# Summing the attention's two output halves in DRAM with an adding transfer

## The chip, the cores and the metric

The kernel runs on one core of a Trainium2 chip. Its engines are TensorE (PE in the profile; PEld is its weight load), VectorE (DVE), ScalarE (ACT), GpSimd (POOL) and SyncE (SP); each works through its own instructions in the order in which the program lists them, and waits on semaphores for the others. Sixteen DMA engines move data; SP and POOL issue the transfers, each on a queue of its own. The metric is the device time of one execution in microseconds, taken as the median of several runs.

## What is computed

One block of a sequence model on 1024 positions of width 1024: a norm, an input projection, two mixers (an mLSTM and a sparse attention, "NSA"), their gated sum through two branch weights, an output projection, and a gated feed-forward part. The change touches the result of the attention and the place where it is used:

```python
def block(i):                      # 64 queries t, 8 heads in 2 groups
    ...
    p_c = masked_softmax(lc, cmp_end[None, :] <= t[:, None])    # compressed keys
    o_c = jnp.einsum('bgrqc,bgcd->bgrqd', p_c, vc_)
    ...
    p_s = masked_softmax(ls, mask_s[:, :, None])                # selected blocks
    o_s = jnp.einsum('bgrqn,bgqnd->bgrqd', p_s, v_g)
    ...
    p_w = masked_softmax(lw, mask_w)                            # window of 512
    o_w = jnp.einsum('bgrqk,bgkd->bgrqd', p_w, v_wb)
    return gb[..., 0:1] * o_c + gb[..., 1:2] * o_s + gb[..., 2:3] * o_w

y_n = nsa_mixer(...)
ys = jnp.stack([y_m, y_n], axis=2)
branch = jnp.einsum('btnw,nwd->btnd', ys, w_branch[l])
mixed = jnp.sum(jax.nn.sigmoid(merge) * branch, axis=2)
```

## The kernel before

All matrix products work on numbers that are split in two: a rounded high part (made on ACT) and the rest, the low part (made by a subtraction on DVE or POOL). A product of two split operands takes three matmuls (`mm3`, L351 to L353).

**The attention** (names in the trace: S, E, T, obank, os) runs over 32 units: four head pairs p, and in each eight tiles i of 128 queries. Unit 13, for example, is tile 5 of pair 1, and unit 16 the first of pair 2. For each unit and each of the two heads, PE forms the logits (S16w and S16s are the window and block logits of unit 16; L1430, L1431), DVE adds the bias and takes the row extremes (L1457), ACT takes the exponential (L1461), and DVE or ACT scales (L1482). The compressed keys have a tile of their own, E16c for unit 16, whose unused columns POOL fills with zeros (L1449) before PE transposes it. PE transposes all of it in groups (T, L1512), ACT and DVE split them (TH, TL), and PE multiplies with the values, accumulating in obank (L1532, L1534). The values are stored as 64 columns of high parts beside 64 columns of low parts, so the accumulated output of a unit is a tile of 128 partitions, of which partitions 0 to 63 hold the product with the high parts and partitions 64 to 127 the one with the low parts. The result is the sum of the two halves, which lie on different partitions.

At the end of a unit ACT copies this tile to the output tile os (L1540; two buffers in turn), and SP stores its halves into two DRAM arrays, d_yn[0][p] and d_yn[1][p] (L1542). The order of the work on PE, ACT and DVE comes from a planner in the kernel, which places operations by estimated costs; POOL and SP simply get their instructions as the planner emits the operations that issue them. When the last logits of a pair are done, `load_pair` issues the loads for the next pair: q on POOL's queue (L1286, L1287; tiles S), on every second pair k too (L1294; tiles R and S, followed by two copies, L1282), and the bias rows on SP's queue (L1301, from d_rep). PE fills its spare time in the attention with dense tiles of the merge gates (d, L351 to L353), whose weights are split into whi on ACT (L331) and wlo on POOL (L333), and whose results ACT evicts (mg, L1387).

**The branch inputs.** Behind the attention, `load_y` (L1814 to L1826) brings eight inputs of 128 x 1024 for the branch products, two transfers each into a ring of six buffers: for k below 4 the mLSTM's output and its gate, which DVE multiplies, and for k of 4 to 7 the two attention halves, which DVE adds (L1820). Each input is then split into YH (ACT, L347) and YL (DVE, L348). This runs beside the last three dense tiles; step k issues the loads of input k and works on input k - 2. Behind the dense tiles PE forms the branch products (br), which need all of YH and YL and the branch weights, of which the first is split (whi, wlo) in the midst of this work. Later stages (output projection, feed-forward part) come from a second planner, and nothing in them is touched.

Of the kernel before, what the change touches and what calls it, by code (L numbers as in the profile page):

```python
# [11 lines left out]
ALU = mybir.AluOpType  # L12
PSUM = bass.MemoryType.PSUM

P = 128
# [26 lines left out]
def cast32(ap):  # L42
    return ap.bitcast(F32)
# [129 lines left out]
def body(ctx, tc, a, out):  # L173
    nc = tc.nc
# [111 lines left out]
    d_so = [tc.dram_tile([P, T], F32, name=f"d_so{j}") for j in range(4)]  # L286
    d_ym = [tc.dram_tile([P, T], F32, name=f"d_ym{j}") for j in range(4)]
    d_yn = [[tc.dram_tile([P, T], F32, name=f"d_yn{z}{j}") for j in range(4)] for z in range(2)]
# [57 lines left out]
    def split_evict(hi, lo, src):  # L346
        nc.scalar.activation(hi, src, AF.Copy)  # L347
        nc.vector.tensor_tensor(lo, src, cast32(hi), ALU.subtract)  # L348

    def mm3(ps, ah, al, bh, bl, first, last):  # L350
        nc.tensor.matmul(ps, ah, bh, start=first, stop=False)  # L351
        nc.tensor.matmul(ps, ah, bl, start=False, stop=False)  # L352
        nc.tensor.matmul(ps, al, bh, start=False, stop=last)  # L353
# [917 lines left out]
    def vhl(i, n):  # L1271
        return vat(4 * i + n)
# [119 lines left out]
    with ExitStack() as sc:  # L1392
# [97 lines left out]
        def t_groups(u):  # L1490
            p, i = units[u]
            bl = [(2, k) for k in range(nwin(i))]
            gr = [(0, bl[z:z + 2]) for z in range(0, len(bl), 2)] + [(0, [(0, 0)])]
            bl = [(1, k) for k in range(i + 1)]
            gr += [(1, bl[z:z + 2]) for z in range(0, len(bl), 2)]
            return gr
# [4 lines left out]
        def t_job(u, gi, grp, last):  # L1501

            p, i = units[u]
            g = p // 2
            if gi == 0:
                PO[u] = [None, 0, sum(len(x[1]) for x in t_groups(u))]
            m = len(grp)
            pt = psC.tile([P, 2, 2 * P], F32, name=f"T{u}_{gi}", tag="T", bufs=2)
            for z, (b, kb) in enumerate(grp):
                for r in range(2):  # L1510
                    e = EX[u, "c"][:, r, :] if b == 0 else EX[u, "w" if b == 2 else "s", r][:, P * kb:P * kb + P]
                    nc.tensor.transpose(pt[:, z, P * r:P * r + P], e, ident)  # L1512
            hl = []

            def high():
                hl.append(cp.tile([P, 2, 2 * P], F32R, name=f"TH{u}_{gi}", tag="TH", bufs=NTH))
                nc.scalar.activation(hl[0][:, 0:m], pt[:, 0:m], AF.Copy)  # L1517

            def low():
                hl.append(cp.tile([P, 2, 2 * P], F32R, name=f"TL{u}_{gi}", tag="TL", bufs=NTH))  # L1520
                nc.vector.tensor_tensor(hl[1][:, 0:m], pt[:, 0:m], cast32(hl[0])[:, 0:m], ALU.subtract)  # L1521

            def pv():
                th, tl = hl
                st = PO[u]
                po = obank[:, u % 2, :]
                for z, (b, kb) in enumerate(grp):
                    if b == 0:
                        vv = VHC[:, g, :]
                    else:  # L1530
                        vv = vhl(kb + (max(0, i - 4) if b == 2 else 0), 2 * (b - 1) + g)
                    nc.tensor.matmul(po, vv, th[:, z, :], start=(st[1] == 0), stop=False)  # L1532
                    st[1] += 1
                    nc.tensor.matmul(po, vv, tl[:, z, :], start=False, stop=(st[1] == st[2]))  # L1534
                if last:
                    os_ = cp.tile([P, 256], F32, name=f"os{u}", tag="os", bufs=2)

                    def out_copy():

                        nc.scalar.activation(os_, po, AF.Copy)  # L1540
                        for z in range(2):
                            nc.sync.dma_start(d_yn[z][p].rearrange("(r d) t -> d r t", r=2)[:, :, P * i:P * i + P],  # L1542
                                              os_[64 * z:64 * z + 64, :].rearrange("d (r t) -> d r t", r=2))
                    return out_copy
                return None

            return 2 * m * 107.0, high, low, pv
# [122 lines left out]
        def ready(op, eng):  # L1670
            t = 0.0
            for d in op.deps:
                d = dep_op(d)
                if isinstance(d, tuple):
                    e = pair_at.get(d[1])
                else:
                    e = d.end
                    if e is not None and d.eng != eng:
                        e += LAT
                if e is None:  # L1680
                    return None
                t = max(t, e)
            if op.extra is not None and len(talloc) >= 2:
                e = talloc[-2].end
                if e is None:
                    return None
                t = max(t, e + LAT)
            return t
# [31 lines left out]
        while any(queues.values()):  # L1720
            best = None
            for e in queues:
                cand = None
                for op in queues[e][:LOOK[e]]:
                    r = ready(op, e)
# [31 lines left out]
            if e == "DVE" and op in s_free:  # L1757
                p = units[op.prio[0]][0]
# [13 lines left out]
    def q1_tile(n, dt):  # L1772
        if n not in q1 or q1[n].dtype != dt:
            q1[n] = q1p.tile([P, 4, 512], dt, name=f"q1_{n}_{len(q1)}", tag=f"q1_{n}", bufs=1)
        return q1[n]
# [24 lines left out]
    with ExitStack() as se:  # L1800
        dp = se.enter_context(tc.tile_pool(name="stD", bufs=1, reuse_waits="tile"))
        psD = se.enter_context(tc.tile_pool(name="psD", bufs=1, space=PSUM, reuse_waits="tile"))
        YH = dp.tile([P, 8, T], F32R, name="YH")
        YL = dp.tile([P, 8, T], F32R, name="YL")
        def load_y():

            ring = [q1_tile(n, F32)[:, 2 * z:2 * z + 2, :].rearrange("p a c -> p (a c)") for n in (4, 0, 1) for z in range(2)]
            ys, loads = {}, 0
            for k in range(10):
                ys[k] = []  # L1810
                for src in ([d_ym[k], d_so[k]] if k < 4 else [d_yn[0][k - 4], d_yn[1][k - 4]]) if k < 8 else []:
                    ys[k].append(ring[loads % 6])
                    loads += 1
                    nc.sync.dma_start(ys[k][-1], src[:, :])  # L1814
                if k > 1:
                    y, *more = ys.pop(k - 2)
                    if k < 6:
                        nc.scalar.activation(more[0], more[0], AF.Sigmoid)
                    for y2 in more:
                        nc.vector.tensor_tensor(y, y, y2, ALU.mult if k < 6 else ALU.add)  # L1820
                    for half in range(2):
                        hs = slice(512 * half, 512 * half + 512)
                        split_evict(YH[:, k - 2, hs], YL[:, k - 2, hs], y[:, hs])
                yield

        ly = load_y()  # L1826
        for j in range(MG1, 16):
            for z, _ in enumerate(merge_tile(j, gring, psD, 8)):
                if z % 4 == 1:
                    next(ly, None)  # L1830
        for _ in ly:
            pass
        for d in range(8):
            n = j_br[d]
            wh, wl = ws.get(n)
            for half in range(2):
                hs = slice(512 * half, 512 * half + 512)
                sg = []
                for b in range(2):
                    gg = gring.tile()  # L1840
                    nc.sync.dma_start(gg, d_mg[8 * b + d][:, hs])
                    nc.scalar.activation(gg, gg, AF.Sigmoid)
                    sg.append(gg)
                for b in range(2):
                    ps = psD.tile([P, 512], F32, name=f"br{d}{half}{b}", tag="D", bufs=8)
                    for k in range(4):
                        kk = 4 * b + k
                        mm3(ps, wh[:, kk, :], wl[:, kk, :], YH[:, kk, hs], YL[:, kk, hs], k == 0, k == 3)
                    nc.vector.tensor_tensor(sg[b], ps, sg[b], ALU.mult)
                if d < 7 and half == 0:  # L1850
                    ws.dma(n + 2)
                    ws.split(n + 1)
                if d == 6 and half == 1:
                    ws.split(n + 2)
                if d == 7:
                    ws.split(n + 3 if half == 0 else n + 4)
                nc.vector.tensor_tensor(sg[0], sg[0], sg[1], ALU.add)
                split_evict(UTH[:, d, hs], UTL[:, d, hs], sg[0])
# [385 lines left out]
    for gi, pairs in enumerate(GROUPS):  # L2244
        ra, rb = {}, {}
        for z in range(2):
            for p in pairs:
                t = 2 * p + z
                ra[p, z] = load2(d_gu[t][:, :], [gub[t]])
                rb[p, z] = load2(wdn[P * t:P * t + P, :])  # L2250
        for q in QS:
# [32 lines left out]
            for j in range(4):  # L2284
                d = acc[q, j]
# [18 lines left out]
    for r in (1, 0):  # L2304
        for j in range(4):
            i = 2 * j + r
# [69 lines left out]
```

## Time and profile before

| | us |
|---|---|
| median of 3 runs (1571.67 to 1578.49) | 1574.69 |
| the profiled execution | 1576.46 |
| its span, first to last instruction | 1574.7 |
| PE busy | 1529.6 |
| DVE busy | 1175.1 |
| ACT busy | 782.0 |
| POOL busy | 126.7 |

The span is 1.8 us shorter than the profiled execution, which has some time around its first and last instruction. The mean granted clock of TensorE over the span is 0.991 of full speed.

In rows of a timeline the first number is the start in us from the span's start, the second the busy time, then engine, line, operation, and output <- inputs; in brackets stands the idle time before it and what ended it. Rows of waits give total us, how often, and the longest. Rows of transfers give their number, the KB of one and the median us from issue to landing.

### The profile page before, as it was taken

To read this page: it belongs to the slowest core of one execution; us is meant where nothing else is said; L and a number is where in the kernel's file an instruction comes from. 1 tells how busy PE (TensorE), PEld (TensorE's weight loads), DVE (VectorE), ACT (ScalarE), POOL (GpSimd) and SP (SyncE) were. 2 spreads that over 40 slices of the span, in tenths; PEclk is the share of its full clock that TensorE was granted. 3 is DMA by queue.
4 is the path that set the end of the run, shared out by engine and by line. 5 is a ranking of instruction groups with operands and counts; after the bars stand their busy time and mean duration, and the time that the engine had idled before them with its cause. 6 is when DMAs were issued, how large, how long until landed. Compare 5 with 4: busy or idle time off the path is not lost.

```text
span 1574.7 us, 22067 instructions
## 1 busy us (share of the span) xinstructions
PE 1529.6 (97%) x7714; PEld 1291.2 (82%) x7714; DVE 1175.1 (75%) x2467; ACT 782.0 (50%) x1668; POOL 126.7 (8%) x184
## 2 busy tenths in 40 slices
PE   6999999998999999998999999999999999999998
PEld 5877888886989888986888888888888888888876
DVE  6978888855888688856564597666666666978996
ACT  6325665653788688865443253333333333454443
POOL 2000000022111211001000041000000000000120
PEclk9999999999999999999999999999999999999999
DMA  8424655599142914137556222222322223650202
GB/s 272 125 75 135 214 182 155 176 241 233 40 112 54 172 40 113 48 101 254 153 176 206 75 67 87 80 81 84 132 92 81 81 88 127 253 215 0 107 1 107
DMA packets 162839, 198.21 MB, mean 126 GB/s; under 512 B 9944, under 2 KB 121974, under 8 KB 162728
## 3 DMA queue, kind: packets, MB, share of 16 engines
q1 hardware_dynamic: 150840, 183.06, 36.5%
q0 software_dynamic: 11600, 13.09, 5.0%
q8 instruction: 61, 1.00, 0.3%
q10 hardware_dynamic: 288, 0.66, 0.1%
q14 instruction: 50, 0.41, 0.1%
HBM read 146.34 MB, written 58.29 MB: 130 GB/s over the span
## 4 chain that ended last, share of the span: by engine, by line
PE 85%; DVE 7%; DMA 5%; ACT 2%; issue 1%; SPq 0%; POOL 0%; DVEq 0%; ACTq 0%; POOLq 0%
PE PS L352 15%; PE PS L353 15%; PE PS L351 15%; PE bk L351 4%; PE bk L352 4%; PE bk L353 4%; PE T L1512 4%; PE obank L1534 2%; PE d L351 2%; PE obank L1532 2%; PE d L353 2%; PE d L352 2%; PE br L353 2%; PE br L351 2%; PE br L352 2%; DMA d_ql<-S 1%
## 5 line engine op out<-in xcount | busy, mean ns | idle before, releaser
L1877 DVE TENSOR_TENSOR sl<-PS,sl 128x512 f32<-128x512 f32 x182 | 123.0, 687 | 99.7 <-PE PS L353 97.7
L1521 DVE TENSOR_TENSOR TL<-T,TH 128x512 fp32r<-128x512 f32 (+1 forms) x184 | 103.3, 582 | 29.1 <-ACT TH L1517 28.3
L1517 ACT ACTIVATE TH<-T 128x512 fp32r<-128x512 f32 (+1 forms) x184 | 90.2, 510 | 28.7 <-PE T L1512 25.7
L1880 ACT ACTIVATE sl<-sl 128x512 f32<-128x512 f32 (+1 forms) x85 | 53.3, 631 | 71.7 <-PE PS L352 46.3
L1877 DVE TENSOR_TENSOR sl<-sl,sl 128x512 f32<-128x512 f32 (+1 forms) x111 | 75.2, 686 | 15.4 <-ACT sl L1880 11.8
L351 PE MATMUL bk<-UTH,op 128*128 128x512 f32 x192 | 77.5, 403 | 1.6 <-ACT S L779 1.6
L1880 ACT ACTIVATE wh<-sl 128x512 fp32r<-128x512 f32 x61 | 38.5, 631 | 81.5 <-PE PS L352 69.1
L353 PE MATMUL bk<-UTH,op 128*128 128x512 f32 x192 | 75.1, 391 | 0.0
L352 PE MATMUL bk<-UTL,op 128*128 128x512 f32 x192 | 75.0, 391 | 0.0
L351 PE MATMUL d<-UTH,whi 128*128 128x512 f32 x176 | 71.9, 409 | 1.4 <-ACT mg L1387 0.7
L353 PE MATMUL d<-UTH,wlo 128*128 128x512 f32 x176 | 69.3, 394 | 1.4 <-POOL wlo L333 1.4
L352 PE MATMUL d<-UTL,whi 128*128 128x512 f32 x176 | 69.1, 393 | 0.0
L351 PE MATMUL PS<-q 128*128 128x512 f32 x172 | 67.0, 390 | 0.0
L352 PE MATMUL PS<-q 128*128 128x512 f32 x172 | 67.0, 390 | 0.0
L353 PE MATMUL PS<-q 128*128 128x512 f32 x172 | 67.0, 390 | 0.0
L1880 ACT ACTIVATE q<-sl 128x512 fp32r<-128x512 f32 x74 | 43.3, 624 | 45.9 <-PE PS L352 30.1
L351 PE MATMUL bk<-T,op 128*128 128x512 f32 x144 | 58.3, 405 | 0.0
L353 PE MATMUL bk<-T,op 128*128 128x512 f32 x144 | 56.4, 391 | 0.0
L352 PE MATMUL bk<-T,op 128*128 128x512 f32 x144 | 56.3, 391 | 0.0
L351 PE MATMUL br<-YH,whi 128*128 128x512 f32 x128 | 50.8, 397 | 2.2 <-ACT whi L331 2.2
L353 PE MATMUL br<-YH,wlo 128*128 128x512 f32 x128 | 50.8, 397 | 2.2 <-POOL wlo L333 2.2
L1877 DVE TENSOR_TENSOR wh<-sl,wh 128x512 fp32r<-128x512 f32 x58 | 39.7, 685 | 15.3 <-ACT wh L1880 15.3
(1377 smaller groups left out, 4854.6 us busy)
## 6 DMA issues: line engine op xcount, KB each, us to landing
rp<-in_w_in SPq DMA_DIRECT2D x22, 512.0 KB, 4.6
ra<-in_w_gate SPq DMA_DIRECT2D x22, 512.0 KB, 4.0
d_gu<-sl SPq DMA_DIRECT2D x44, 256.0 KB, 2.0
q<-d_mg SPq DMA_DIRECT2D x32, 256.0 KB, 2.9
d_rep<-d_row SPq DMA_DIRECT2D x8, 960.0 KB, 7.4
sl<-d_gu SPq DMA_DIRECT2D x15, 512.0 KB, 5.3
sl<-in_w_down SPq DMA_DIRECT2D x15, 512.0 KB, 4.3
ra<-in_w_up SPq DMA_DIRECT2D x11, 512.0 KB, 3.5
```

The source lines that it names most:

```text
L351: nc.tensor.matmul(ps, ah, bh, start=first, stop=False)
L352: nc.tensor.matmul(ps, ah, bl, start=False, stop=False)
L353: nc.tensor.matmul(ps, al, bh, start=False, stop=last)
L1512: nc.tensor.transpose(pt[:, z, P * r:P * r + P], e, ident)
L1517: nc.scalar.activation(hl[0][:, 0:m], pt[:, 0:m], AF.Copy)
L1521: nc.vector.tensor_tensor(hl[1][:, 0:m], pt[:, 0:m], cast32(hl[0])[:, 0:m], ALU.subtract)
L1532: nc.tensor.matmul(po, vv, th[:, z, :], start=(st[1] == 0), stop=False)
L1534: nc.tensor.matmul(po, vv, tl[:, z, :], start=False, stop=(st[1] == st[2]))
L1877: return pl.step(alts, lambda e: ENG[e].tensor_tensor(out_(), x(), y(), alu), reads, writes, **kw)
L1880: return pl.step((("ACT", cost),), lambda e: nc.scalar.activation(out_(), x(), fn), reads, writes, **kw)
```

## The change

The two stores of a unit now go to the same array, d_yn[0][p]. The first half is stored by SP as before. The second half is sent by POOL's queue with an accumulating transfer, which adds to what lies in DRAM. Since it reads and writes what the first has written, it waits until that has landed. `load_y` then loads one array for each attention input instead of two, and there is nothing left to add on DVE.

```diff
                         for z in range(2):
-                            nc.sync.dma_start(d_yn[z][p].rearrange("(r d) t -> d r t", r=2)[:, :, P * i:P * i + P],
-                                              os_[64 * z:64 * z + 64, :].rearrange("d (r t) -> d r t", r=2))
+                            kw = {"accum_op": ALU.add} if z else {}
+                            (nc.gpsimd if z else nc.sync).dma_start(d_yn[0][p].rearrange("(r d) t -> d r t", r=2)[:, :, P * i:P * i + P],
+                                              os_[64 * z:64 * z + 64, :].rearrange("d (r t) -> d r t", r=2), **kw)
...
-                for src in ([d_ym[k], d_so[k]] if k < 4 else [d_yn[0][k - 4], d_yn[1][k - 4]]) if k < 8 else []:
+                for src in ([d_ym[k], d_so[k]] if k < 4 else [d_yn[0][k - 4]]) if k < 8 else []:
```

The order of PE is the same, row for row; ACT's too. On POOL the 32 adding transfers come in between. Before, POOL's list around the loads of pair 2 reads (d_qh, d_ql, d_kh, d_kl are the stored high and low parts of q and k; KHC and KLC those of the compressed keys):

```order
L1449 MEMSET E14c 128x97 x2
L1449 MEMSET E15c 128x89 x2
L1286 DMA S_2_2827<-d_qh_133 64x1024
L1287 DMA S_2_2827<-d_ql_137 64x1024
L1286 DMA S_2_2844<-d_qh_133 64x1024
L1287 DMA S_2_2844<-d_ql_137 64x1024
L1294 DMA R_1_2959<-d_kh_128 64x8x128 x2
L1294 DMA R_1_2959<-d_kl_130 64x8x128 x2
L1294 DMA S_2_2920<-d_kh_127 64x1024 x2
L1294 DMA S_2_2921<-d_kl_129 64x1024 x2
L1282 COPY R_1_2959<-KHC 128x8x64
```

Now, from the same fill of E15c on, with os_5121 the output of unit 13 (waits left out):

```order
L1449 MEMSET E15c 128x89 x2
L1543 DMA d_yn_148<-os_5121 64x2x128
L1286 DMA S_2_2827<-d_qh_133 64x1024
L1287 DMA S_2_2827<-d_ql_137 64x1024
L1286 DMA S_2_2844<-d_qh_133 64x1024
L1287 DMA S_2_2844<-d_ql_137 64x1024
L1294 DMA R_1_2959<-d_kh_128 64x8x128 x2
L1294 DMA R_1_2959<-d_kl_130 64x8x128 x2
L1294 DMA S_2_2920<-d_kh_127 64x1024 x2
L1294 DMA S_2_2921<-d_kl_129 64x1024 x2
L1282 COPY R_1_2959<-KHC 128x8x64
```

The loads of the pair now stand behind the adding transfer of unit 13, which cannot be issued before unit 13 has ended and its first half has landed. The loads of pair 1 and pair 3 stand in the same way behind units 5 and 21. A little further on, the list now reads (os_5256 and os_5349 are the outputs of units 14 and 15):

```order
L1282 COPY R_1_2959<-KLC 128x8x64
L333 TENSOR_TENSOR wlo_5226<-raw_4612,whi_5225 128x1024
L1543 DMA d_yn_148<-os_5256 64x2x128
L1543 DMA d_yn_148<-os_5349 64x2x128
L1449 MEMSET E16c 128x121 x2
```

Before, the fill of E16c stood right behind the low part wlo_5226; two adding transfers came between them.

On SP, the loads of the attention inputs before (d_yn_147 to d_yn_150 are the first halves of the four pairs, d_yn_151 to d_yn_154 the second; the stores of d_mg are the evicted merge gates):

```order
L1388 DMA d_mg_198<-q_5_0_7539 512x1x128
L315 DMA raw_7635<-in_w_branch 128x8x128
L1814 DMA q_0_2_7558<-d_yn_147 128x1024
L1814 DMA q_0_2_7558<-d_yn_151 128x1024
L1814 DMA q_1_3_7559<-d_yn_148 128x1024
L1814 DMA q_1_3_7559<-d_yn_152 128x1024
L1388 DMA d_mg_199<-q_5_0_7539 512x1x128
L1814 DMA q_4_1_7557<-d_yn_149 128x1024
L1814 DMA q_4_1_7557<-d_yn_153 128x1024
L1814 DMA q_0_2_7558<-d_yn_150 128x1024
L1814 DMA q_0_2_7558<-d_yn_154 128x1024
```

And now:

```order
L1388 DMA d_mg_198<-q_5_0_7539 512x1x128
L315 DMA raw_7635<-in_w_branch 128x8x128
L1815 DMA q_0_2_7558<-d_yn_147 128x1024
L1815 DMA q_0_2_7558<-d_yn_148 128x1024
L1388 DMA d_mg_199<-q_5_0_7539 512x1x128
L1815 DMA q_1_3_7559<-d_yn_149 128x1024
L1815 DMA q_1_3_7559<-d_yn_150 128x1024
```

The two groups of four loads, ahead of and behind a store, have become two groups of two, and each takes one buffer of the ring instead of two.

## The prediction

> **What bounds the kernel now.** I read the page's busy shares first, then the chain of work that ended last, then the attention and the branch stage stretch by stretch.
>
> ```profile
> span 1574.7 us, 22067 instructions
> PE 1529.6 (97%) x7714; PEld 1291.2 (82%) x7714; DVE 1175.1 (75%) x2467; ACT 782.0 (50%) x1668; POOL 126.7 (8%) x184
> PE 85%; DVE 7%; DMA 5%; ACT 2%; issue 1%; SPq 0%; POOL 0%; DVEq 0%; ACTq 0%; POOLq 0%
> ```
>
> TensorE is busy for 97% of the span and carries 85% of the chain, so work taken from VectorE or from a queue is worth only the TensorE gaps that end on it. The change touches the attention (about 377 to 710 us, where the halves are written) and the loading of the branch inputs (about 699 to 738 us, where they are read). Busy time by stretch:
>
> ```profile
> 510.00:590.00 80.00, 79.53 (x514) 70.40 (x513) 61.16 (x198) 60.94 (x163) 15.97 (x29) 1.00 0.56 110
> 590.00:710.00 120.00, 116.95 (x761) 103.92 (x761) 88.66 (x279) 93.91 (x238) 11.79 (x25) 1.00 0.31 91
> 730.00:745.00 15.00, 10.67 (x37) 7.80 (x36) 7.99 (x10) 6.71 (x11) 3.13 (x1) 0.77 0.76 237
> ```
>
> The columns are length, then busy us of PE, PEld, DVE, ACT and POOL, granted clock, DMA share and GB/s. The attention has almost nothing to give; it can only lose. The branch stage has 4.33 us of idle PE in 15, at a mean granted clock of 0.77. Its waits, from 700 to 760 us:
>
> ```profile
> PE br L353 <- POOL wlo L333: 2.2, 1, 2.2
> PE br L351 <- ACT whi L331: 2.2, 1, 2.2
> PE d L353 <- POOL wlo L333: 1.4, 1, 1.4
> ```
>
> The first two stand one behind the other before the branch products; the third is earlier and stems from the inputs of the mLSTM, which the change leaves alone. What leads to them is in the timelines of ACT, DVE, POOL and SP:
>
> ```profile
> 723.18 0.67 ACT L1387 ACTIVATE q<-d,COLS 128x512 f32<-128x512 f32 x1
> 731.83 1.15 ACT L347 ACTIVATE YH<-q 128x512 fp32r<-128x512 f32 x2 [1.72 <-DVE q L1820]
> 732.88 1.04 ACT L331 ACTIVATE whi<-raw 128x1024 fp32r<-128x1024 f32 x1
> 730.57 1.23 DVE L1820 TENSOR_TENSOR q<-q 128x1024 f32<-128x1024 f32 x1 [0.24 <-DMA q<-d_yn]
> 734.00 3.13 POOL L333 TENSOR_TENSOR wlo<-raw,whi 128x1024 fp32r<-128x1024 f32 x1 [12.99 <-ACT whi L331]
> 715.50 3.68 SPq L1814 DMA_DIRECT2D q<-d_yn  x4
> 724.51 3.88 SPq L1814 DMA_DIRECT2D q<-d_yn  x4
> ```
>
> Read upwards: the branch weight's low part (734.00 to 737.13) waits for its high part on ACT, which stands behind the rounding of the seventh input, which waits for the addition of its two halves, which waits for the eight loads.
>
> **The clock behind that stall.** The windows are cut where the clock's record steps:
>
> ```profile
> 730.82:734.23 3.41, 1.26 (x6) 0.76 (x5) 2.71 (x4) 2.10 (x3) 0.23 (x1) 1.00 0.98 317
> 734.23:741.05 6.82, 4.64 (x11) 3.14 (x11) 3.35 (x3) 2.30 (x4) 2.90 (x1) 0.50 0.53 155
> 355.35:358.76 3.41, 1.81 (x8) 1.20 (x7) 0.98 (x2) 1.73 (x4) 0.00 (x0) 1.00 1.35 343
> 925.37:928.78 3.41, 1.65 (x13) 1.21 (x11) 3.41 (x5) 1.62 (x3) 2.83 (x2) 1.00 0.00 0
> ```
>
> The stretch of 3.41 us with 1.26 us of PE work, and the one with 1.65, are the last before a halving of 6.8 us; the one with 1.81 is not. So about 1.7 us of idleness inside one such stretch brings a halving, at up to 3.4 us. The stall at 731.82 paid for one: from there to 741.05 (9.23 us) PE did 0.26 + 4.64 x 0.5 = 2.58 us of full-speed work, so **6.65 us** were lost. The Trainium skill ("TensorE: Matmul & The Clock Gate", part 1) has half clock after an idle window of about 3.4 us. Read as a wholly idle window, that would not tie this halving to a stall of 2.15 us and would leave only the idle 4.33 us to win, a gain below of 2.8 us in place of 5; the two rows with 1.26 and 1.65 us of work speak against that reading.
>
> **The change part by part.** *The reading end.* Eight loads of 512 KB become four, and four additions of 1.23 us go. The ACT order there stays as it is: evict, inputs five and six, evict, input seven, weight, input eight. With both five and six landed during the wait before 722, ACT goes on from 723.85 (723.18 + 0.67) with two roundings of 1.15 and an evict of 0.67, to 726.8. Input seven is loaded at 724.5 as now, but as the first of two transfers, not of four. Rows for its landing:
>
> ```profile
> q<-d_yn SPq DMA_DIRECT2D x8, 512.0 KB, 6.2
> q<-d_ym SPq DMA_DIRECT2D x4, 512.0 KB, 4.6
> ```
>
> I take 4.6, since fewer transfers queue: landed at 729.1, rounded by 730.3, weight's high part by 731.3, low part (2.40 us when VectorE leaves it alone, below; 3.13 at worst) by 733.8 to 734.5. The dense tiles end at 731.82, the first two products of the branch take 0.46, so PE idles about 1.5 us where it idled 4.33, just short of the halving. Lost 1.5 in place of 6.65: **5 us won**. Worst of the pieces (6.2 landing, 3.13) idles 3.8 us and halves again: 0 to 1.5 won. Best: no idling, and the 1.4 us wait goes too: 8.0.
>
> *The writing end.* 32 stores leave SP (0.6 us of issue each, in a queue with idle time between) and become 32 adding transfers on POOL's queue. Each waits for the first store of its unit to land, and what stands behind it on POOL waits too.
>
> ```profile
> d_yn<-os SPq DMA_DIRECT2D x64, 64.0 KB, 2.1
> L1286 POOL DMA_DIRECT2D S<-d_qh x8: 512/522/653, 334.1 to 593.2; - x8
> ```
>
> So an adding transfer starts 2.1 us behind its store and takes POOL about 0.6. Behind it stand, by the order listing: zero fills of the compressed probabilities, which the transposes need, weight low parts of the dense tiles, and the loads of q and k for the next head pair. Fills and low parts have cover; the tightest is the fill of unit 16, now 532.75, then behind the adding transfer of unit 15 (its store is at 541.53, so 544.2), for the transposes at 548.13: 3.4 us to spare. Without that cover each costs its lateness.
>
> ```profile
> 541.53 1.23 SPq L1542 DMA_DIRECT2D d_yn<-os  x2
> 532.75 0.33 POOL L1449 MEMSET E16c<- 128x121 f32 x2
> 548.13 0.27 PE L1512 MATMUL T<-cst,E16c 128*128 128x128 f32 x1
> ```
>
> The loads of a pair have less. For pair 2 they now start at 508.80 and 519.90; behind the adding transfer of unit 13, whose store is at 523.23, q starts at about 526, and twelve issues (4 x 0.52, 4 x 0.68, 4 x 0.52) follow back to back to 533, the last four held until the first q have landed, as they reuse their semaphores.
>
> ```profile
> 508.80 0.54 POOL L1286 DMA_DIRECT2D S<-d_qh  x1
> 519.90 1.39 POOL L1294 DMA_DIRECT2D R<-d_kh  x2 [9.02 <-PE S15w L1431]
> 523.23 1.23 SPq L1542 DMA_DIRECT2D d_yn<-os  x2
> 530.41 2.40 POOL L333 TENSOR_TENSOR wlo<-raw,whi 128x1024 fp32r<-128x1024 f32 x1 [2.27 <-ACT whi L331]
> 524.00:532.00 8.00, 8.00 (x51) 6.90 (x50) 6.67 (x17) 6.98 (x15) 5.01 (x7) 1.00 1.70 224
> 532.00:541.00 9.00, 8.96 (x61) 7.71 (x60) 3.29 (x7) 3.75 (x8) 1.26 (x5) 1.00 1.12 278
> 543.67 0.25 PE L1430 MATMUL S16w<-R,S 128*128 128x192 f32 x1
> 545.41 0.22 PE L1430 MATMUL S16s<-S,S 128*128 128x128 f32 x1
> ```
>
> The DMA engines are full from 524 to 541 already (share above 1) at 224 to 278 GB/s. Now about 2.1 MB (q and half of k, eight transfers of 256 KB) that went before come into this rush of bias rows, weights and the other k. In all 5.3 MB (a weight tile of 0.5, bias rows 1.7, q 1.0, k 2.1) from 525 on end at 546.2 at 250 GB/s, 544.1 at 278, 548.7 at 224; q and the first k, ahead in their queue, near 543. S16w at 543.67 just has them; S16s at 545.41 waits for the last k, which needs up to 2.1 us more to be reported: between 0 (at 278) and 5.4 (at 224, last in line). I take **2 us**, from the middle rate and half of the 2.1; 3.4 more if the clock falls. For pair 1, q alone (1 MB, 4 us at the same rate, 8 where the bias rows take half) starts at 451, 2.7 us behind the store of unit 5, and is used at 460.46: 0, at most 2. Pair 3 stands in the same way.
>
> ```profile
> 448.24 1.22 SPq L1542 DMA_DIRECT2D d_yn<-os  x2
> 460.46 0.25 PE L1430 MATMUL S8w<-R,S 128*128 128x192 f32 x1
> ```
>
> *The adding transfer itself* stands in no row. The nearest:
>
> ```profile
> S<-d_kl POOLq DMA_DIRECT2D x2, 256.0 KB, 11.4
> L1540 ACT ACTIVATE os<-obank x32: 362/384/386, 397.2 to 696.8; 128x256 f32<-128x256 f32 x32
> ```
>
> Below, 2.1 us like the plain store; above, 11.4, a POOL load landing in the full rush. Two units on, ACT needs the output tile back. The 32 copies are 9.7 us apart in the mean (299.6 / 31), two of them 19, and 2.7 go before the adding transfer is out, so a landing of up to 16 us is covered on average. I take 3 us, near the plain store, as the bytes are the same 64 KB: 0 cost at either end.
>
> **Sum:** -5 + 2 = -3 us. The profiled execution took 1576.46 (span 1574.7), so 1573.5 on its footing; it lies 1.8 above the median of 1574.69, so the forecast for the median is **1572**.
>
> **The rivals.** *Forecast, within 0.5%* (7.9 us, about what a measurement of this kernel can tell from no change): 0.70, with the gain anywhere from 0 to 7. *Late loads, slower:* the k loads of pair 2 land at 553, PE stands at S16s for 8 us and gets the half clock, and pair 1 adds 2: 8 + 3.4 + 2 - 5 = +8, 1583, and more beyond. It decides where the last k load lands more than 7.5 us past 545.4. For it: the full DMA engines; against: even at the slow 224 GB/s the bytes are through by 549. 0.10. *Slow adds, slower:* from a landing of 16 us on, ACT's copy waits for its tile, and PE behind it; at 20 us that is 4 us for every two units, 16 x 4 = 64, or 1635. No row speaks for it: 0.05. *Starved issue, slower:* VectorE's scalings hold POOL's descriptors back; 2.5 us for each of 13 issues would put pair 2 32 us late, 1600. The issue rows (522 ns median, 653 at most, in the same stage) speak against it: 0.03. The Trainium skill ("SBUF — State Buffer", the "DVE blocks DMA" trap) warns of this, with about 620 ns becoming 3100; by that rule this rival would be the forecast, and the 653 ns disagree. *All of the tail and no loss, faster:* 8.0 won and no lateness, 1566.7, or luck with the clock elsewhere: 0.12.
>
> **Chances and range.** Faster 0.12, same 0.70, slower 0.18. The range takes in the best tail (-8, and some run-to-run spread) below and the late loads with one halving (2 to 11 us late, less the gain) above: 1564 to 1585.
>
> **What would show it.** Right: the loads' rows show four d_yn, no additions; the branch's two waits together under 2 us and no half clock near 735; a wait of S16s for a DMA of 0 to 5 us near 545. Wrong: waits on POOL in the T lines (fills late), ACT idle before the output copy (adds slow), POOL issues above 1 us (starved), or a halving near 545. A larger gain than 8 us would mean a wait that I have not seen.

## The result, and the profile after

| | before | after |
|---|---|---|
| median of 5 runs, us (range) | 1574.69 (1571.67 to 1578.49) | 1584.57 (1581.8 to 1587.61) |
| the profiled execution, us | 1576.46 | 1584.63 |
| ratio after to before, 95% interval | | 1.0061 (1.0041 to 1.0080) |

The changed kernel is slower by 0.6%, 9.6 us by the ratio. The forecast was 1572, within 0.5% of before; the time lies inside the range of 1564 to 1585, but it went up, which was not the forecast. The page of the changed kernel, its span, busy shares and chain:

```profile
span 1582.8 us, 22087 instructions
PE 1529.8 (97%) x7714; PEld 1290.5 (82%) x7714; DVE 1171.8 (74%) x2463; ACT 782.1 (49%) x1668; POOL 160.0 (10%) x216
PE 82%; DVE 7%; DMA 7%; ACT 2%; issue 1%; POOL 0%; SPq 0%; DVEq 0%; ACTq 0%; POOLq 0%
```

PE and ACT do what they did, DVE 3 us less. In the chain DMA goes from 5% to 7% and PE from 85% to 82%. Which transfers are meant stands in PE's waits from 380 to 770 us (total, how often, longest; the rows on a transfer, on mg and on POOL):

```profile
PE d L351 <- ACT mg L1387: 4.5, 2, 4.1
PE S8w L1430 <- DMA S<-d_ql: 3.6, 2, 3.1
PE S24w L1430 <- DMA S<-d_ql: 1.8, 2, 1.4
PE br L353 <- POOL wlo L333: 0.9, 1, 0.9
PE d L353 <- POOL wlo L333: 0.9, 1, 0.9
```

Before, S8w and S24w had no such row, and that for mg was

```profile
PE d L351 <- ACT mg L1387: 0.7, 2, 0.4
```

The losses lie at the three changes of head pair: S8w is the first work of pair 1, S24w of pair 3, and the long wait for mg falls in the first unit of pair 2. The last two rows are what remains of the branch stage's waits. In the kernel before, the first load of q for pair 1 was issued at

```profile
431.95 0.55 POOL L1286 DMA_DIRECT2D S<-d_qh  x1 [0.29 <-issue]
```

The timeline of POOL now, at this first pair change, with the two PE rows that end the wait:

```profile
449.41 0.96 POOL L1543 DMA_DIRECT2D d_yn<-os  x1 [10.76 <-DMA d_yn<-os]
450.03 0.94 POOL L1286 DMA_DIRECT2D S<-d_qh  x1
...
451.64 0.91 POOL L1287 DMA_DIRECT2D S<-d_ql  x1
459.70 0.33 PE L1430 MATMUL S8w<-R,S 128*128 128x192 f32 x1 [0.49 <-DMA S<-d_ql]
463.24 0.53 PE L1430 MATMUL S8w<-R,S 128*128 128x192 f32 x1 [3.10 <-DMA S<-d_ql]
```

POOL stood until the first half of unit 5 had landed, issued its adding transfer, and the loads of q only then, at 450.0 to 451.6. They took 7.0 to 11.6 us to land (3.4 to 5.3 before), and PE waited for the last of them. At the second pair change the same queue gives 12 loads from 533.09 on, where the kernel before began at 508.80; this time the victim is a store. SP and ACT of the same kernel:

```profile
541.73 0.54 SPq L1388 DMA_DIRECT2D d_mg<-mg  x1
554.12 0.69 ACT L1387 ACTIVATE mg<-d,COLS 128x512 f32<-128x512 f32 x1 [6.15 <-DMA d_mg<-mg]
```

The store of a merge gate, issued at 541.73, was reported only at 554.1, 12.4 us later (2.5 is the median of such a store). There is one buffer mg, so the next eviction waited, and PE behind it. The windows around the two stalls and the branch stage (length, busy us of PE, PEld, DVE, ACT, POOL, clock, DMA share, GB/s), cut where the clock's record steps:

```profile
458.08:461.49 3.41, 1.57 (x12) 1.22 (x10) 1.86 (x7) 1.97 (x6) 0.00 (x0) 1.00 1.18 264
461.49:468.32 6.83, 5.08 (x20) 4.69 (x21) 1.20 (x8) 1.23 (x6) 2.18 (x2) 0.50 0.64 139
550.23:553.65 3.42, 0.50 (x5) 0.33 (x3) 0.68 (x8) 0.00 (x0) 0.00 (x0) 1.00 1.31 225
553.65:560.48 6.83, 5.62 (x16) 4.76 (x17) 2.07 (x13) 3.20 (x14) 1.51 (x5) 0.50 0.53 129
742.00:757.00 15.00, 14.12 (x63) 11.37 (x62) 6.80 (x8) 6.96 (x11) 2.38 (x1) 1.00 0.76 231
```

Each of the two stalls paid for 6.83 us at half clock besides. The last row is the branch stage: 0.88 us of idle PE in 15, where it had 4.33 and a halving.

So the account of the profiled execution by these rows is: pair 1, 3.6 us of waiting and 5.08 / 2 = 2.5 of half clock; pair 2, 4.1 and 5.62 / 2 = 2.8; pair 3, 1.8; together 14.8 us lost.

PE's order is the same in both kernels, so each matmul can also be set beside its twin, and its lateness read off (one row of S10w, behind pair 1: 470.06 before, 475.90 now). Taken so, the changed kernel falls back by 7.3 us at pair 1, by 0.8 at a wait for VectorE near 506, by 6.1 at pair 2 and by 2.3 at pair 3, 16.5 in all, and gains 6.4 at the branch stage (700 to 760 us before). That leaves 10.1 us; the spans differ by 8.1. The rest are halvings at other places, which fall differently in each profiled execution: the kernel before has two near 929 and 1530 that the changed one lacks, and lacks one near 837 that the changed one has.

### The profile page after: what moved, and what is told of

The parts are those of the page before. It is cut to its first block, busy times and chain, and to the rows that moved or that the text cites. A ratio compares the mean times of both kernels' runs of the same rounds, so it can differ in the third digit from the quotient of the medians.

```text
span 1582.8 us, 22087 instructions
## 1 busy us (share of the span) xinstructions
PE 1529.8 (97%) x7714; PEld 1290.5 (82%) x7714; DVE 1171.8 (74%) x2463; ACT 782.1 (49%) x1668; POOL 160.0 (10%) x216
## 4 chain that ended last, share of the span: by engine, by line
PE 82%; DVE 7%; DMA 7%; ACT 2%; issue 1%; POOL 0%; SPq 0%; DVEq 0%; ACTq 0%; POOLq 0%
PE PS L352 15%; PE PS L351 15%; PE PS L353 15%; PE bk L351 4%; PE bk L352 4%; PE bk L353 4%; PE T L1512 3%; PE obank L1532 2%; PE obank L1534 2%; PE d L351 2%; PE d L353 2%; PE d L352 2%; PE br L353 2%; PE br L351 1%; PE br L352 1%; DMA d_ql<-S 1%
## 5 line engine op out<-in xcount | busy, mean ns | idle before, releaser
L1543 POOL DMA_DIRECT2D d_yn<-os x32 | 32.3, 1010 | 240.7 <-ACT TH L1517 38.9
L1878 POOL TENSOR_TENSOR acc<-acc 128x512 f32<-128x512 f32 x4 | 5.9, 1501 | 493.0 <-DVE acc L1878 493.0
```

Source lines behind the costliest of these rows:

```text
L1543: (nc.gpsimd if z else nc.sync).dma_start(d_yn[0][p].rearrange("(r d) t -> d r t", r=2)[:, :, P * i:P * i + P], os_[64 * z:64 * z + 64, :] ...
L1878: return pl.step(alts, lambda e: ENG[e].tensor_tensor(out_(), x(), y(), alu), reads, writes, **kw)
```

## The experiments

Every ratio below is to the kernel before, which ran beside the experiments at 1572.41 us (11 runs, the first four kernels) and 1572.82 us (27 runs, the other four). The changed kernel did not run beside them; its 1.0061 is to the kernel before of its own runs, 1574.69.

**The reading end alone.** The two stores as before, but only the first array loaded:

```diff
-                for src in ([d_ym[k], d_so[k]] if k < 4 else [d_yn[0][k - 4], d_yn[1][k - 4]]) if k < 8 else []:
+                for src in ([d_ym[k], d_so[k]] if k < 4 else [d_yn[0][k - 4]]) if k < 8 else []:
```

> The kernel before with its two stores as they were, and only the reading end of the change: the attention's inputs of the branch are loaded from the first array alone, without the addition (the sum leaves out the products with the values' low parts). This measures the reading end by itself. Theory P: as in the changed kernel, PE's idle time between 731 and 748 falls from 4.3 us to under 2 us, no halving near 735, and the time is 5 to 7 us under that of the kernel before, 1568 to 1570 (ratio 0.995 to 0.997). Theory C (the gain there was phase): the time stays within 2 us of the kernel before.

Measured: 1566.14 us, ratio 0.9955 (0.9942 to 0.9968). PE's waits from 700 to 760 us:

```profile
PE d L353 <- POOL wlo L333: 1.5, 1, 1.5
PE br L353 <- POOL wlo L333: 1.1, 1, 1.1
```

The two waits of 2.2 have become one of 1.1, and no halving stands there in the clock's record. The reading end is worth 7.1 us (5.0 to 9.1) by itself. Matmul by matmul, 5.5 us of the gain of the profiled execution lie at the branch stage; the rest there are halvings elsewhere, of which this execution has fewer. With the change at 1.0061 the writing end costs 1.06%, or 16.7 us (13 to 20 by the two intervals), and that is what the other runs take apart.

**A plain store in the adding transfer's place**, in the same order and with the same wait:

```diff
-                            kw = {"accum_op": ALU.add} if z else {}
+                            kw = {}
```

> The changed kernel with the second store of a unit still on GpSimd's queue, to the same addresses and behind the same wait for the first half, but as a plain store in place of an adding one; the sum then leaves out the products with the values' high parts. Theory P (place): all waits stay, S8w near 460 2 to 3.5 us, mg near 554 3 to 4.5 us, S24w near 633 1 to 2 us, and the time is 1582 to 1587. Theory A (the addition): the waits fall by half or more, and the time is 1572 to 1577. Theory C (phase): waits like those of the changed kernel, time anywhere from 1575 to 1587 by where the halvings fall.

Measured: 1584.07 us, ratio 1.0072 (1.0060 to 1.0085); S8w waited 1.9 us, mg 4.6, S24w 1.0. These waits lie in the ranges of theory P or within 0.1 us of them, and matmul by matmul the three pairs lose 6.1, 6.0 and 1.9 us. So without any addition the loss is about the same: what costs is the place and the wait, not the reading and adding in DRAM. Theory A falls. The groups of the transfer's issues on POOL (ns, least, median, most), first of this kernel:

```profile
L1543 POOL DMA_DIRECT2D d_yn<-os x32: 597/612/756, 398.9 to 713.0; - x32
```

and of the changed kernel:

```profile
L1543 POOL DMA_DIRECT2D d_yn<-os x32: 942/977/1322, 398.8 to 714.8; - x32
```

An adding transfer shows 0.98 us on POOL, a plain one 0.61. But the load behind it starts 0.62 us later in the changed kernel (449.41, 450.03) and 0.59 later with the plain store (449.54, 450.13): the longer row overlaps the next.

**Only the second half's store on POOL's queue.** The kernel before with this one edit; the store goes to its own array and waits for no other:

```diff
-                            nc.sync.dma_start(d_yn[z][p].rearrange("(r d) t -> d r t", r=2)[:, :, P * i:P * i + P],
+                            (nc.gpsimd if z else nc.sync).dma_start(d_yn[z][p].rearrange("(r d) t -> d r t", r=2)[:, :, P * i:P * i + P],
```

> The kernel before with only one edit: the second half's store goes from SyncE's queue to GpSimd's, as a plain store into its own array; the reading end is that of before. It waits for the copy on ACT but not for the first half's landing, so the pair loads stand behind it some 2.7 us less late than in the changed kernel. Theory P (place): q of pair 1 issued near 447 and of pair 2 near 530; the wait at S8w 0 to 1 us, at the eviction of mg near 552 1 to 4 us, at S24w 0; no gain near 735, so 1575 to 1583. Theory A: no adding transfer, so no loss, 1573 to 1576, with waits under 0.5 us at all three places.

Measured: 1580.86 us, ratio 1.0057 (1.0040 to 1.0073), so 9.0 us lost of the 16.7. The rows of waits:

```profile
PE S24w L1430 <- DMA S<-d_ql: 2.4, 1, 2.4
PE S16w L1431 <- DMA R<-d_kl: 1.7, 1, 1.7
PE S16s L1431 <- DMA S<-d_kl: 1.1, 1, 1.1
PE S16s L1430 <- DMA S<-d_kh: 0.5, 1, 0.5
```

The place in the queue is enough for about half of the loss, without an addition and without a wait for the first half; the time fits theory P. Matmul by matmul, nothing is lost at pair 1, 4.9 us at pair 2 and 4.3 at pair 3. These victims are not theory P's: I expected none at S24w, and mg at pair 2, where the k loads themselves came late. q of pair 1 was issued at 447.6, 2.4 us earlier than in the changed kernel, and S8w did not wait.

**The adding transfers two units later.** They are kept in a list, and `add_half` issues the oldest of it just before ACT's copy takes the output tile again:

```diff
                 if last:
+                    if u > 1:
+                        add_half()
                     os_ = cp.tile([P, 256], F32, name=f"os{u}", tag="os", bufs=2)
...
+                            if z:
+                                late.append((dst, src))
```

> The changed kernel, but the adding transfer of a unit is given to GpSimd's queue only two units later, just before ACT's copy needs the output tile again. Nothing is taken out; the pair loads then stand behind the adding transfers of units 3, 11 and 19, whose first halves landed long before. Theory P (place): the loss is the pair loads' lateness, because they stand behind an adding transfer that still waits for its unit and its first half. Then q of pair 1 is issued before 445 instead of 450, of pair 2 near 509 instead of 533, of pair 3 well before 623; the waits at S8w (3.1 us), at the eviction of mg near 554 (4.1 us) and at S24w (1.4 us) fall under 0.5 us each, the halvings of the clock near 461 and 553 go, the gain near 735 stays, and the time is 1566 to 1571 (ratio 0.994 to 0.998 of the kernel before). Theory A (the adding transfer itself): its issue of 1.0 us and its reading and writing of DRAM cost the time wherever it stands; then the time stays at 1581 or above. Theory C (the phase of the clock's windows): the loss is luck; then the waits change little and the time is anywhere from 1572 to 1585.

Measured: 1581.27 us, ratio 1.0059 (1.0046 to 1.0072), where theory P had 0.994 to 0.998. The three waits went as it said (none at S8w or S24w, 0.4 at mg near 540), but a new one came. PE's waits from 520 to 560 us (in this kernel obank stands at L1538, ACT's copy at L1548, the adding transfer at L1503):

```profile
PE obank L1538 <- ACT os L1548: 6.9, 1, 6.9
```

The timelines of POOL and ACT show what leads there:

```profile
528.73 2.39 POOL L333 TENSOR_TENSOR wlo<-raw,whi 128x1024 fp32r<-128x1024 f32 x1 [2.27 <-ACT whi L331]
531.07 2.04 POOL L1503 DMA_DIRECT2D d_yn<-os  x2
538.12 0.38 ACT L1548 ACTIVATE os<-obank 128x256 f32<-128x256 f32 x1 [8.40 <-DMA d_yn<-os]
```

Two units late, the adding transfer of unit 12 came to stand behind the loads of pair 2, their copies and a low part, at 531.07; it landed in the rush, and ACT's copy of unit 14 waited 8.4 us for the tile. A smaller wait for mg, 1.8 us near 642, is new too. The time alone would have spoken for theory A or C; the rows say that the edit had moved the wait to the other side of the same loads. That left open whether every place near a pair change costs as much (theory V), which the next run was made for.

**One unit later.** The same with `if u > 0`: the loads of a pair stand behind the adding transfers of units 4, 12 and 20, whose first halves have landed by then or soon will, and the adding transfer of unit 12 no longer stands behind the loads of pair 2.

> As the run with the adding transfers two units later, but only one unit later: the pair loads stand behind the adding transfers of units 4, 12 and 20, and unit 12's is no longer behind the loads of pair 2, their copies and a low part. Theory P (place): the loss lies in what the queue holds back, in the first case the pair loads, in the two-unit case the adding transfer of unit 12, on which ACT's copy of unit 14 waited (6.9 us of PE). Then no wait over 1 us at S8w, at the eviction of mg near 550, at S24w, or of obank for os; no halving near 461, 537 or 553; and the time is 1565 to 1569 at a kernel before of 1572.4 (ratio 0.995 to 0.998). Theory V (a crowded stretch): around each pair change the DMA engines and GpSimd's queue are so full that 32 more transfers there always make something late; then a new wait of 3 us or more stands between 520 and 560, and the ratio is 1.002 or more.

Measured: 1569.08 us, ratio 0.9971 (0.9958 to 0.9984). The longest of PE's waits from 380 to 770 us on a transfer, on mg, or on POOL:

```profile
PE d L351 <- ACT mg L1387: 1.4, 2, 1.1
PE br L353 <- POOL wlo L333: 1.0, 1, 1.0
PE d L353 <- POOL wlo L333: 0.9, 1, 0.9
```

The timelines of POOL and ACT at the second pair change:

```profile
510.73 1.15 POOL L1503 DMA_DIRECT2D d_yn<-os  x1 [6.15 <-DMA d_yn<-os]
511.35 1.09 POOL L1286 DMA_DIRECT2D S<-d_qh  x1
538.77 0.38 ACT L1548 ACTIVATE os<-obank 128x256 f32<-128x256 f32 x1 [3.62 <-DMA d_yn<-os]
```

All 32 adding transfers are there, q of pair 2 is issued at 511.35 where it was 533.09 in the change, the waits at S8w and S24w are gone, and no halving stands between 362 and 818 us. The 1.1 us at mg is just above the 1 us of theory P. Theory V falls. So does C, by this run and the next two: the edits take waits away, and the time goes with them, over 12, 12 and 9 runs. And this kernel is faster than both: 0.9% below the change, 0.3% below the kernel before. So 0.90 of the 1.06% that the writing end cost are back; the intervals are too wide to tell whether the rest is. The place is not without a risk: the last row is ACT's copy of unit 15, which waits 3.6 us for the adding transfer of unit 13, now behind the loads of pair 2. PE did not wait for it.

**One pair change at a time.** The changed kernel, with the adding transfer of unit 13 alone one unit later:

```diff
+                    if u == 14:
+                        add_half()
...
+                            if z:
+                                late.append((dst, src))
+                                if u != 13:
+                                    add_half()
```

> The changed kernel, in which the adding transfer of unit 13 alone is given to the queue one unit later, so that the loads of pair 2 stand behind that of unit 12; pairs 1 and 3 are left as in the change. Theory P: the wait of PE for mg near 554 (4.1 us) and its halving (0 to 3.4 us, 1.7 in the profiled run) go and those of pair 1 and pair 3 stay: 4 to 7 us under the changed kernel, ratio 1.0015 to 1.0035 of the kernel before. Theory V: another wait takes the place; ratio 1.005 or more.

and with that of unit 5 alone (the same edit with 5 for 13 and 6 for 14):

> The changed kernel, in which the adding transfer of unit 5 alone is given to the queue one unit later, so that the loads of pair 1 stand behind that of unit 4. Theory P: the wait at S8w (3.1 us) and its halving (3.4 us of work lost) go, those of pair 2 and 3 stay: 5 to 7 us under the changed kernel, ratio 1.0015 to 1.003. Theory V: another wait takes the place; ratio 1.005 or more.

Measured: 1.0030 (1.0016 to 1.0044) and 1.0029 (1.0017 to 1.0041). Each takes about 5 us off the change (1.0061 less 1.0030 and less 1.0029, of 1573 us), and by the intervals anything from 1 to 9. The rows of waits, of the first:

```profile
PE S8w L1430 <- DMA S<-d_ql: 3.4, 2, 3.1
PE S24w L1430 <- DMA S<-d_ql: 1.1, 1, 1.1
PE d L351 <- ACT mg L1387: 0.9, 2, 0.6
```

and of the second:

```profile
PE d L351 <- ACT mg L1387: 4.2, 2, 3.8
PE S24w L1430 <- DMA S<-d_ql: 0.8, 1, 0.8
PE T L1518 <- DVE E8w L1482: 1.1, 1, 1.1
```

Each edit removes its own wait and leaves the other one: the two are independent. In the second run a shorter wait, the row of E8w, came in the first unit of pair 1; otherwise nothing took their place. The lateness against the kernel before that the matmuls gain shows it place by place (us, over the matmuls that stand at 440 to 470, 520 to 560, 610 to 640 and 700 to 760 us in the kernel before):

| | pair 1 | pair 2 | pair 3 | branch stage |
|---|---|---|---|---|
| the change | 7.3 | 6.1 | 2.3 | -6.4 |
| unit 13 alone one unit later | 7.2 | 0.3 | 1.4 | -5.8 |
| unit 5 alone one unit later | 1.8 | 4.9 | 1.1 | -6.2 |
| all one unit later | 0.0 | 0.8 | 0.0 | -6.3 |

So the move of a single queue entry, 64 KB, is worth 5 to 6 us in the profiled execution. The two together account for 0.63 of the 0.90% between the change and the run with all of them late; how much of the other 0.27% is pair 3 can't be said from the times, since the intervals are as wide as that.

**Is the store of mg held by its own queue?** SP's queue had taken 1.7 MB of bias rows 8 to 10 us ahead of it. The change with this store on ACT's queue:

```diff
-            nc.sync.dma_start(parity(d_mg[j], half), st.rearrange("p (j c) -> p j c", c=P))
+            nc.scalar.dma_start(parity(d_mg[j], half), st.rearrange("p (j c) -> p j c", c=P))
```

> The changed kernel, with the stores of the evicted merge gates (d_mg from mg, 18 of 256 KB) issued on ACT's queue instead of SyncE's. In the changed kernel one such store, issued at 541.7 behind 1.7 MB of bias rows on SyncE's queue, took some 12 us to land, and the next eviction waited for it. Theory Q (the queue): it was slow because it stood behind the bias rows in its own queue; on ACT's queue it lands within 5 us, the wait near 554 falls under 1 us, S16s takes at most 1 us in its place, and the ratio is 1.002 to 1.004. Theory D (the engines): the sixteen DMA engines are shared and full, so it lands as late from any queue; the wait stays 3 to 5 us, ratio 1.005 to 1.008.

Measured: 1586.38 us, ratio 1.0092 (1.0074 to 1.0110). ACT's timeline with that store and the next eviction:

```profile
537.43 0.52 ACTq L1388 DMA_DIRECT2D d_mg<-mg  x1
551.00 0.69 ACT L1387 ACTIVATE mg<-d,COLS 128x512 f32<-128x512 f32 x1 [6.65 <-DMA d_mg<-mg]
```

PE's wait from 530 to 565 us:

```profile
PE d L351 <- ACT mg L1387: 4.6, 1, 4.6
```

ACT's queue had nothing ahead of the store, and still the eviction that waits for it goes on 13.6 us after the issue, no sooner than with SP's queue (12.4). Theory Q falls, and theory D, the shared DMA engines, is left for this wait; with unit 13 late, where the loads came earlier, it fell to 0.6 us. The time lies above theory D's range, though. That this kernel is slower than the change itself was in neither theory and stays open; its trace shows PE's waits at the T lines for TL at 4.5 us, where the change had 2.3.

## Why the prediction failed, step by step

**The reading end, -5: right.** Alone it gives 7.1 us (5.0 to 9.1), in the change 6.4 by the matmuls. Its pieces hold too. The rows of transfers after:

```profile
q<-d_yn SPq DMA_DIRECT2D x4, 512.0 KB, 4.8
d_yn<-os POOLq DMA_DIRECT2D x32, 64.0 KB, 2.8
S<-d_qh POOLq DMA_DIRECT2D x8, 256.0 KB, 9.1
```

An input of the branch lands in 4.8 us (taken 4.6; the last row, q of a pair, belongs to pair 1 below and had 4.7 before), the low part took 2.38 (2.40), PE idles 0.88 (1.5), and the halving that went with the stall went.

**The adding transfer itself, 0: right.** It lands in 2.8 us in the median (taken 3; 7.9 at most), and no copy waited for it in the change. The cover of some 16 us was an average, though: the least time between its landing and the copy that takes the tile again was 5.2 us.

**The fills and low parts, 0: right.** No wait on POOL stands at a T line.

**Pair 1, "0, at most 2": the step that failed first.** It lost 7.3 us, 6.1 of them in the rows of its wait and its halving. I had q's 1 MB take 4 us, or 8 "where the bias rows take half". But the store of mg (0.26 MB), the bias rows (1.70) and a weight tile (0.52) are issued within the same 3 us, and q, at 1.05, is through only when nearly all of it is. Of GpSimd's queue (q0) and SP's (q1), the packets from 450 to 463.2 us were (number, MB, share of the 16 engines):

```profile
q1 hardware_dynamic: 1389, 2.11, 68.5%
q0 software_dynamic: 464, 1.11, 37.8%
```

That is 3.23 MB at 244 GB/s, and S8w went on at 463.24, when the last of q had landed. The sum that I did for pair 2, done here, gives 3.53 MB, which from 450.0 at 278 to 224 GB/s end at 463 to 466 (an estimate, from those rates of the prediction): it would have shown the lateness. **Pair 3**, "the same way", lost 2.3, 1.8 of them in the row of S24w.

**Pair 2, "I take 2 us", at S16s: the lateness right, the victim and the size wrong.** It lost 6.1 us by the matmuls (6.9 by the rows). q was issued when I had said: 533.09 is 526.6 on the clock of the kernel before, since this one was 6.5 us behind by then. But S16w and S16s waited for no load. I counted the bytes that PE needs and asked when they land; I did not ask what else was in flight. The store of mg has one buffer and went into the same rush. The half clock, which I held ready as "3.4 more", came at both places and cost 5.3 us.

So in place of -5 + 2 the two ends came to -6.4 and +16.5, and it is the second term that was wrong: the three pairs, put at 2 us together, lost 15.7.

**The rivals.** "Late loads" had the mechanism and nearly the time (1583), at 0.10. That its time came so close is luck: it put 11.4 us at pair 2 and 2 at pair 1, where 6.1 and 7.3 were lost. Its deciding point, the last k load 7.5 us past 545.4, decided nothing; what I set against it (the bytes are through by 549) was about the loads and didn't speak for the store. Two of the signs of being wrong showed: a halving near 545 (it came at 553.65), and issues above 1 us on POOL, the sign of "starved issue", where the row shows up to 1322 ns. The issues are not starved: loads start every 0.5 to 0.6 us as before, and with plain stores the rows are short and the time is the same. The Trainium skill's rule ("SBUF — State Buffer", the "DVE blocks DMA" trap), by which a transfer from GpSimd's queue takes about 3100 ns in place of 620 beside a copy on VectorE, does not explain this loss. "Slow adds" did not come.

**The clock.** The stretches of 3.41 us ahead of the two new halvings hold 1.57 and 0.50 us of PE work. With the rows of the prediction (1.26 and 1.65 lead to a halving, 1.81 does not) this again puts the step near half of a stretch. It is not sharp: with unit 13 alone late, a stretch of 1.63 us (385.10 to 388.50) had no halving behind it, and with the plain store on POOL's queue one of 1.80 (544.07 to 547.49) had one. The Trainium skill ("TensorE: Matmul & The Clock Gate", part 1) has an idle window of about 3.4 us; the window here need not be idle, only less than about half busy.

## What to carry to other kernels

A transfer that waits must be priced by what stands behind it in its queue, not by its own bytes: here 64 KB held back 1 to 3 MB of loads, and issuing it one unit later, where its wait is over, turned 0.6% lost into 0.3% won in this kernel. Where late loads meet others, add up every byte in flight, stores of single buffers too, and take the moment at which the whole sum is through; then ask whose buffer is needed first. A delay that is free in one place can block a buffer in another, so place it by the queue's order and not by a fixed distance.

## What the runs showed of the hardware

- **A store starved beside loads from another queue.** In the changed kernel the store of mg was issued at 541.73, and the bias rows ahead of it were through by 540. The packets from 541.7 to 545.5 us, all of them GpSimd's but for one of instructions (q14), and of the two queues from 545.5 to 553.9:

```profile
q0 software_dynamic: 1166, 0.79, 234.7%
q14 instruction: 1, 0.01, 1.2%
...
q0 software_dynamic: 1482, 1.62, 124.0%
q1 hardware_dynamic: 807, 0.39, 34.3%
```

ACT's queue fared no better: issued there at 537.43, the store had its first packet at 543.4. It also goes the other way: from 450 to 454 us, at pair 1, SP's queue moved 0.73 MB and GpSimd's 0.09, though q had been issued from 450.03 on. The Trainium skill ("DMA: Bandwidth & Descriptors", section "Issuing engines are not separate DMA queues") says that transfers of all issuers run on the same engines; the 13.6 us on ACT's queue agree.
- **An adding transfer of 64 KB** in pieces of 512 bytes costs POOL a row of 0.98 us, of which 0.62 hold up the queue, and lands in 2.8 us, where the plain one on the same queue took 2.0.
